# Both directions' chunk inverses merged in common groups, a longer patience for tiled groups, and the last two gMLP value blocks ahead of their input blocks

## The chip, the cores and the metric

The kernel runs on one core of one Trainium2 chip. The metric is device microseconds from start to end of the program; the time before is the median of three runs. The engines are named as the profile names them: PE is the matrix engine (PEld its weight loads), DVE the vector engine, ACT the scalar engine, POOL the general engine, SP the one that issues most DMAs.

## The reference, cut to what matters

One layer of a hybrid model runs over 640 tokens (512 of a grid and 128 of a context). One input product feeds two kinds of mixers: a bidirectional recurrence with 16 heads (RWKV-7) and a gated MLP over chunks of 128 tokens (gMLP) with 8 groups.

```python
h = _rmsnorm(x, lp['norm1_g']) * (1.0 + sc1) + sh1
p = h @ lp['w_in']
o_a, s_fin = _rwkv7_bidir(shift_fn(p[..., :C_SHIFT], lp['mu_shift']), s0, lp)
o_b = _chunk_gmlp(jax.nn.gelu(p[..., C_SHIFT:]), lp)
x = x + g1 * (jnp.concatenate([o_a, o_b], axis=-1) @ lp['w_out'])
h = _rmsnorm(x, lp['norm2_g']) * (1.0 + sc2) + sh2
ff = (jax.nn.silu(h @ lp['w_ffn_gate']) * (h @ lp['w_ffn_up'])) @ lp['w_ffn_down']
...
# _rwkv7_bidir, for each of the two directions
sa = jnp.einsum('bhvk,bhk->bhv', S, a_t)
S = S * w_t[:, :, None, :] + sa[..., None] * b_t[:, :, None, :] + v_t[..., None] * k_t[:, :, None, :]
...
# _chunk_gmlp
u, v = jnp.split(p, 2, axis=-1)
vc = v - mean
v = vc * lax.rsqrt(jnp.mean(vc * vc, axis=-1, keepdims=True) + LN_EPS) * lp['gmlp_ln_g'] + lp['gmlp_ln_b']
s = jnp.einsum('gij,bnjgd->bnigd', lp['w_spatial'], v) + lp['b_spatial'].T[:, :, None]
return (u * s.reshape(B, T, D_B)).astype(dtype)
```

## The kernel before

The program has stages. The first makes the modulation vectors for the first norm and the normalized tokens `h_hi`, `h_lo`. The second computes the input product block by block (a block is 128 columns of `w_in`) and, beside it, everything that the recurrence needs ahead of its scan, and the gMLP. The third runs the recurrence over chunks of 64 tokens with half of the output product, the later ones the rest of the output product and the feed-forward network.

In the second stage a block is 96 wide products of 128 x 128 by 320 columns on PE (`big`): 32 triples of high by high, high by low and low by high parts. 40 blocks, 1280 triples, go through the planner below. `fetch` loads a quarter of a block (`raw`), `parted` splits it (`hi`, `lo`), `take` copies the finished block out of PSUM into `praw` and appends the block's own task to a queue.

For each of eight pairs of heads p the blocks are r (`take_r`), v (`take_v`: its transposes `pvt<-ident,zv` go through the buffer `vt` to DRAM) and k (`take_k`, which makes `R` and `X` for each direction d). `tail` makes the Gram products `pG`, `solve` inverts the 16 x 16 diagonal blocks on DVE, and `merge` puts them together to inverses of 64 x 64: per direction five steps of small products on PE in 32 x 32 tiles (`pblk<-TB,A__`, `pblk<-M,TB`, `pblk<-TB,M`, `pM<-TB,GB`, `pT<-TF,M`), each followed by copies or adds out of PSUM, and at the end a store of `TF`. The blocks of gMLP group g are its value block (`take_gv`: a GELU on `praw`, transposes `pvt<-ident,praw`, a layer norm on `vt`, the weight `wspT` from `pw`) and its input block (`take_gu`: a GELU, the products `psp<-wspT,vt`, the sum `sp`, the gate, and a store to `d_o`). `mod_all` makes four more modulation vectors: 64 loads `wt` of 1 MB, each followed by one product group `pm` of four in 128 x 32 tiles; after every 16 the bias rows are loaded to `ms`, added, and transposed (`ptm`). `wt` and `ms` share one buffer.

The order of every engine is written out at build time by `Lister`, a planner with estimated costs. Each queue is a task whose instructions come in sequence (`qA`, `qR`, `qT`, `qM` for the merges, `qB` for the gMLP, and so on), and the wide products are a task that fills PE. A group of another tiling interrupts the wide products only when two such groups are ready, or one has been ready for `PATIENCE`. Once the wide products are written out, what is left is placed by the general scheduler together with the beginning of the third stage. Four accumulators in PSUM (`slots`) serve all groups but the wide ones and `pm`. Every instruction of the second stage is recorded at the line of one helper (L106 before, L109 after), so it is told apart by its tiles.

Of the kernel before, what the change touches and what calls it, by code (L numbers as in the profile page):

```python
# [10 lines left out]
F32 = mybir.dt.float32  # L11
# [8 lines left out]
P = 128  # L20
# [3 lines left out]
NT = T // P  # L24
HALF = T // 2
CH = 64
NCH = T // CH
# [21 lines left out]
SUBST = 4.6  # L49
MODR = 19.0  # L50
TOGETHER = 2
PATIENCE = 2.0
SLACK = 1.0
NREC = 8
CHK = (3, 3, 4, 4, 4, 4)
POOLK = (3,)
# [155 lines left out]


class Task:
    def __init__(self, gen, prio):
        self.gen, self.prio, self.item, self.over = gen, prio, None, False
        self.step()

    def step(self):
# [11 lines left out]
class Lister:  # L231
# [7 lines left out]
        self.wide = Task(wide, 0)  # L239
        self.tasks.append(self.wide)  # L240

    def add(self, gen, prio):
        self.tasks.append(Task(gen, prio))

    def ready(self, ops):
        e, r = ops[0].eng, 0.0
# [36 lines left out]
    def pick(self, eng, tasks):  # L283
        now = self.clock[eng]
        c = [(self.ready(t.item), t.rank(), i, t) for i, t in enumerate(tasks)]
        if eng == "PE":
            small = [x for x in c if x[3] is not self.wide and x[0] + SLACK * (x[3].item[0].tiling != self.tiling or self.tiling == (P, P)) <= now]
            wide = [x for x in c if x[3] is self.wide and x[0] <= now]
            full = [x for x in small if x[3].item[0].tiling == (P, P)]
            if full and self.tiling == (P, P):  # L290
                return now, min(full, key=lambda x: x[1])[3]
            if small and self.tiling != (P, P):
                same = [x for x in small if x[3].item[0].tiling == self.tiling]
                return now, min(same or small, key=lambda x: x[0])[3]
            if small and (not wide or len(small) >= TOGETHER or now - min(small)[0] >= PATIENCE):
                return now, min(small)[3]
            if wide:
                return now, self.wide
        start = min(max(now, x[0]) for x in c)
        return start, min((x for x in c if max(now, x[0]) <= start), key=lambda x: (x[1], x[0], x[2]))[3]  # L300
# [18 lines left out]
def flow_step(ctx: ExitStack, tc, x_prompt, x_sample, state_rwkv, c, c_ctx, w_mod, b_mod,  # L319
# [418 lines left out]
        pass  # L738

    pairs = [Pair() for _ in range(NPAIR)]  # L740

    def take_r(pr, p, read):
        o = pairs[p]
# [201 lines left out]
    vts = [None] * 8  # L945

    def take_gv(vv, g, read):
        lng, lnb, wsp = (gs.tile([P, P], F32, tag=n, name=n) for n in ("lng", "lnb", "wsp"))
        yield oQ.dma_start(lng, gmlp_ln_g[0, g].partition_broadcast(P))
        yield oQ.dma_start(lnb, gmlp_ln_b[0, g].partition_broadcast(P))  # L950
# [17 lines left out]
        va = gs.tile([P, NT], F32, name="gva")  # L968
# [61 lines left out]
    def merge(p, d2):  # L1030

        GB = pairs[p].GB
        for gq in range(8):
            b = 16 * (gq % 2)
            yield oG.dma_start(TB[16 * gq:16 * gq + 16, :, :, :, b:b + 16].rearrange("p d c w b -> p (d c w) b"),
                              d2[gq].rearrange("d c w a b -> a (d c w) b"))
        for h in range(2):
            base = 64 * (1 - h)
            for d in range(2):
                yield oS.copy(A1_[base:base + 16, d, :, 16:32], GB[d][base:base + 16, :, 16:32])  # L1040
                yield oS.copy(A1_[base + 32:base + 48, d, :, 16:32], GB[d][base + 32:base + 48, :, 48:64])
        for d in range(2):
            GBd = GB[d]
            TF = bp.tile([P, NCH, CH], F32, tag="TF", name="TF")
            for h in range(2):
                yield oG.memset(TF[hi32(h), :, 0:32], 0.0)
            Tn, TT, A1 = TB[:, d, :, 0, :], TB[:, d, :, 1, :], A1_[:, d]

            def blk(lhs, rhs, rows=range(4)):
                ps = slots.tile([P, NCH, 32], F32, "pblk")  # L1050
                four = []
                for cc in range(NCH):
                    for a_ in rows:
                        s = slice(32 * a_, 32 * a_ + 32)
                        four.append(oT.matmul(ps[s, cc, :], lhs[s, cc, :], rhs[s, cc, :], start=True, stop=True,
                                             tile_position=(32 * a_, 32 * a_)))
                return ps, four

            M1 = bp.tile([P, NCH, 32], F32, tag="M1", name="M1")
            yield slots.free  # L1060
            ps, four = blk(A1, Tn)
            yield four
            yield oS.copy(M1, ps)
            slots.done(ps)

            yield slots.free
            ps, four = blk(TT, M1, (0, 2))
            yield four
            for h in range(2):
                yield oV.tensor_add(Tn[lo32(h)], ps[lo32(h)], Tn[lo32(h)])  # L1070
            slots.done(ps)
            yield slots.free
            ps, four = blk(M1, TT)
            yield four
            for h in range(2):
                yield oV.tensor_add(TF[lo32(h), :, 0:32], ps[lo32(h)], TT[lo32(h)])
                yield oV.tensor_add(TF[hi32(h), :, 32:64], ps[hi32(h)], TT[hi32(h)])
            slots.done(ps)
            M2 = bp.tile([P, NCH, 32], F32, tag="M1", name="M2")
            yield slots.free  # L1080
            ps = slots.tile([P, NCH, 32], F32, "pM2")
            yield [oT.matmul(ps[hi32(h), cc, :], GBd[lo32(h), cc, 32:64], Tn[lo32(h), cc, :],
                            start=True, stop=True, tile_position=(64 * (1 - h), 64 * (1 - h) + 32))
                   for cc in range(NCH) for h in range(2)]
            for h in range(2):
                yield oS.copy(M2[hi32(h), :, :], ps[hi32(h), :, :])
            slots.done(ps)
            yield slots.free
            ps = slots.tile([P, NCH, 32], F32, "pT2")
            yield [oT.matmul(ps[lo32(h), cc, :], M2[hi32(h), cc, :], TF[hi32(h), cc, 32:64],  # L1090
                            start=True, stop=True, tile_position=(64 * (1 - h) + 32, 64 * (1 - h)))
                   for cc in range(NCH) for h in range(2)]
            for h in range(2):
                yield oS.copy(TF[lo32(h), :, 32:64], ps[lo32(h), :, :])
            slots.done(ps)
            yield oG.dma_start(d_S[p, :, d, :, F_T:F_T + CH], TF)
            merged.append(p)
        yield oG.memset(TB[:, :, :, 0, 0:16], 0.0)

    def mod_all():  # L1100
# [1101 lines left out]
```

## Time and profile before

| what | value |
|---|---|
| median of three runs | 3279.66 us (3274.77 to 3281.91) |
| the profiled execution | 3288.36 us, span 3286.6 us |
| mean granted clock of PE | 0.978 |
| PE busy | 3131.1 us (95%) |
| PE weight loads | 2887.5 us (88%) |
| DVE, ACT, POOL busy | 2378.6, 1441.7, 1255.7 us |
| last wide product of the second stage | issued at 1026.23 us |
| first product of the third stage | issued at 1045.21 us |

PE overlaps its matmuls, so a share of 95% does not mean that it does useful work at its peak for all of that time. A row of the order in time has its start, its duration, the engine, the line, the operation, what it writes and reads, the shape and count, and in brackets how long the engine was idle before it and what ended that. For SP and POOL queues a DMA row is the issue alone; the load lands later.

### The profile page before, as it was taken

The page shows a single profiled execution, that of the slowest core. Times are in us where ns is not written, and L with a number is a line of the kernel's source. Part 1 is how long each engine was busy: PE and PEld are TensorE (multiplying, and loading weights), DVE is VectorE, ACT ScalarE, POOL GpSimd, SP SyncE. Part 2 cuts the span into 40 slices and gives each one's busy share as a digit, 9 for nine tenths or more (in the row PEclk, how much of TensorE's full clock was granted, in tenths as well). Part 3 has the DMA queues.
Part 4 walks back from the last instruction along what each step waited for, and adds up shares of the span by engine and source line. Part 5 has one row for each costly group of instructions (what it writes and reads, how often), then busy time and mean ns, then how long its engine had stood idle before and what let it go on. Part 6 is the DMA issues. An engine that isn't in the chain of part 4 may idle for free.

```text
span 3286.6 us, 73564 instructions
## 1 busy us (share of the span) xinstructions
PE 3131.1 (95%) x28828; PEld 2887.5 (88%) x28828; DVE 2378.6 (72%) x4073; ACT 1441.7 (44%) x3161; POOL 1255.7 (38%) x1082
## 2 busy tenths in 40 slices
PE   6899999999998999899999999999999999999996
PEld 3688888889886877788899999999999999999986
DVE  4456767667665666557877888788887878877787
ACT  3244555555533333245543444444444444444365
POOL 0001222212220122310465565556655645555543
PEclk8899999999997999999999999999999999999998
DMA  8768887887895777456333333433343354554453
GB/s 316 256 181 230 218 229 206 236 217 192 236 232 171 220 231 219 124 157 181 104 115 119 120 106 120 121 116 116 110 124 120 106 175 149 157 167 128 121 167 119
DMA packets 741923, 553.01 MB, mean 168 GB/s; under 512 B 141688, under 2 KB 674184, under 8 KB 732744
## 3 DMA queue, kind: packets, MB, share of 16 engines
q1 hardware_dynamic: 729256, 534.62, 54.7%
q0 software_dynamic: 9984, 13.13, 1.7%
q8 instruction: 226, 3.70, 0.5%
q14 instruction: 121, 0.99, 0.1%
q10 hardware_dynamic: 2336, 0.57, 0.1%
HBM read 438.77 MB, written 111.69 MB: 167 GB/s over the span
## 4 chain that ended last, share of the span: by engine, by line
PE 39%; DVE 6%; issue 5%; DMA 4%; ACT 1%; POOL 1%; DVEq 0%; SPq 0%; ACTq 0%; POOLq 0%
PE P L1816 13%; PE P L1815 12%; PE P L1814 12%; DVE lo L1633 3%; DMA d_os<-act 2%; DVE act L1935 1%; DMA opd<-d_op 1%; ACT hi L1632 1%; DVE xd L1867 0%; PE big L1669 0%; PE big L1668 0%; PE big L1667 0%; DVE xo L1596 0%; PE C L1748 0%; DVE out L2170 0%
## 5 line engine op out<-in xcount | busy, mean ns | idle before, releaser
L1816 PE MATMUL P<-xo,lo 128*128 128x320 f32 x2352 | 732.8, 312 | 13.5 <-DVE lo L1633 13.4
L1814 PE MATMUL P<-xo,hi 128*128 128x320 f32 x2352 | 729.6, 310 | 6.9 <-ACT hi L1632 6.9
L1815 PE MATMUL P<-xo,hi 128*128 128x320 f32 x2352 | 728.4, 310 | 0.0
L1633 DVE TENSOR_TENSOR lo<-raw,hi 128x512 fp32r<-128x512 f32 x532 | 574.9, 1098 | 78.2 <-ACT hi L1632 73.3
L1632 ACT CAST hi<-raw 128x512 fp32r<-128x512 f32 x532 | 326.3, 621 | 414.1 <-PE P L1815 320.1
L1816 PEld LDWEIGHTS P<-xo,lo 128*128 128x128 f32 x2352 | 443.1, 188 | 22.6 <-DVE lo L1633 22.6
L1814 PEld LDWEIGHTS P<-xo,hi 128*128 128x128 f32 x2352 | 443.2, 188 | 9.4 <-ACT hi L1632 9.1
L1815 PEld LDWEIGHTS P<-xo,hi 128*128 128x128 f32 x2352 | 443.1, 188 | 0.0
L106 PE MATMUL big<-h_hi,hi 128*128 128x320 f32 x1280 | 419.3, 328 | 1.0 <-ACT praw L1209 1.0
L1727 POOL TENSOR_TENSOR raw<-raw 128x512 f32<-128x512 f32 x252 | 408.5, 1631 | 11.6 <-DVE lo L1633 1.6
L1816 PE MATMUL P<-xd,lo 128*128 128x320 f32 x1232 | 384.8, 312 | 16.3 <-DVE lo L1633 16.1
L106 PE MATMUL big<-h_lo,hi 128*128 128x320 f32 x1280 | 395.2, 309 | 0.0
L106 PE MATMUL big<-h_hi,lo 128*128 128x320 f32 x1280 | 395.1, 309 | 0.0
L1814 PE MATMUL P<-xd,hi 128*128 128x320 f32 x1232 | 382.7, 311 | 6.2 <-ACT hi L1632 4.1
L1815 PE MATMUL P<-xd,hi 128*128 128x320 f32 x1232 | 381.3, 309 | 0.0
L1632 ACT CAST hi<-rawd 128x512 fp32r<-128x512 f32 (+1 forms) x288 | 168.9, 588 | 239.3 <-PE P L1815 204.6
L1727 POOL TENSOR_TENSOR t<-raw 128x512 f32<-128x512 f32 x84 | 135.6, 1615 | 358.9 <-DMA raw<-in_w_ffn_up_dram 352.0
L106 PEld LDWEIGHTS big<-h_hi,hi 128*128 128x128 f32 x1280 | 241.8, 189 | 32.9 <-issue 26.1
L1816 PEld LDWEIGHTS P<-xd,lo 128*128 128x128 f32 x1232 | 231.9, 188 | 24.0 <-DVE lo L1633 23.5
L106 PEld LDWEIGHTS big<-h_lo,hi 128*128 128x128 f32 x1280 | 241.8, 189 | 1.3 <-issue 0.2
L106 PEld LDWEIGHTS big<-h_hi,lo 128*128 128x128 f32 x1280 | 241.1, 188 | 0.0
L1633 DVE TENSOR_TENSOR lo<-rawd,hi 128x512 fp32r<-128x512 f32 (+1 forms) x288 | 221.8, 776 | 26.1 <-ACT hi L1632 22.3
(370 smaller groups left out, 6275.9 us busy)
## 6 DMA issues: line engine op xcount, KB each, us to landing
wt<-in_w_mod_dram SPq DMA_DIRECT2D x96, 1024.0 KB
raw<-in_w_ffn_gate_dram SPq DMA_DIRECT2D x182, 256.0 KB
raw<-in_w_ffn_up_dram SPq DMA_DIRECT2D x182, 256.0 KB
rec<-d_S SPq DMA_DIRECT2D x80, 576.0 KB
raw<-in_w_in_dram SPq DMA_DIRECT2D x172, 256.0 KB
rawd<-in_w_ffn_down_dram SPq DMA_DIRECT2D x128, 256.0 KB
raw<-in_w_out_dram SPq DMA_DIRECT2D x96, 256.0 KB
xd<-d_os SPq DMA_DIRECT2D x66, 320.0 KB
```

Of the source, the lines that this page charges most:

```text
L106: self.eng, self.run = eng, lambda: fn(*args, **kw)
L1632: S.copy(hi[:, 0:nk], raw[:, 0:nk])
L1633: V.tensor_sub(lo[:, 0:nk], raw[:, 0:nk], hi[:, 0:nk].bitcast(F32))
L1727: G.tensor_tensor(out=o[:, 0:nk], in0=p[:, 0:nk], in1=q[:, 0:nk], op=ALU.subtract)
L1814: TE.matmul(ps, hi[:, k, :], xk[:, 0, :], start=f, stop=False)
L1815: TE.matmul(ps, hi[:, k, :], xk[:, 1, :], start=False, stop=False)
L1816: TE.matmul(ps, lo[:, k, :], xk[:, 0, :], start=False, stop=l)
L1935: V.tensor_sub(lo, src, hi.bitcast(F32))
```

## The change

Merging runs once per pair. Each of the five steps of `merge` issues the products of both directions as one group, into two accumulators taken together, and the copies and adds of both follow; the two `TF` buffers are `TF` and `vt`, which the value transposes of `take_v` use too, so a list `held` lets only one of the two users in at a time. `PATIENCE` goes from 2 to 3 for all tasks (it becomes a property of a task, with the same value for all). In `take_gv` the offset `lnb` is loaded later, into the buffer of `wsp`, and group 7 gets buffers of its own for `wspT` and `vt`, the latter once all pairs have passed. The blocks of groups 6 and 7 come in the order value 6, value 7, input 6, input 7.

```diff
-PATIENCE = 2.0
+PATIENCE = 3.0
+PACE = 3.0
+PATM = 3.0
+PATT = 3.0
...
-            if small and (not wide or len(small) >= TOGETHER or now - min(small)[0] >= PATIENCE):
+            if small and (not wide or len(small) >= TOGETHER or any(now - x[0] >= x[3].patience for x in small)):
...
+        yield lambda: not held
+        held.append(p)
         vt = bp.tile([P, NT, P], F32, tag="vt", name="vt", bufs=1)
         yield from turned(o.zv, vt, "pvt")
         yield oQ.dma_start(d_vt[p, 0].rearrange("(q t) v -> t q v", t=P), vt)
+        held.pop()
...
-        wspT = gs.tile([P, P], F32, name="wspT")
+        wspT = (bk if g == 7 else gs).tile([P, P], F32, tag="wlr" if g == 7 else "wspT", name="wspT", bufs=1)
         yield oS.copy(wspT, pw[:, 0, :])
         slots.done(pw)
-        vt = bp.tile([P, NT, P], F32, tag="vt2", name="vt2", bufs=1)
+        lnb = gs.tile([P, P], F32, tag="wsp", name="lnb")
+        yield oQ.dma_start(lnb, gmlp_ln_b[0, g].partition_broadcast(P))
+        if g == 7:
+            yield lambda: done["zv"] == NPAIR
+        vt = bp.tile([P, NT, P], F32, tag="t2" if g == 7 else "vt2", name="vt2", bufs=1)
...
-        for d in range(2):
-            GBd = GB[d]
-            TF = bp.tile([P, NCH, CH], F32, tag="TF", name="TF")
...
+        two = lambda: [slots.tile([P, NCH, 32], F32, "pblk") for d in range(2)]
+
+        def blk(ps, lhs, rhs, rows=range(4)):
+            return [oT.matmul(ps[d][s, cc, :], lhs[d][s, cc, :], rhs[d][s, cc, :], start=True, stop=True,
+                             tile_position=(s.start, s.start))
+                    for d in range(2) for cc in range(NCH) for s in (slice(32 * a_, 32 * a_ + 32) for a_ in rows)]
+
+        yield slots.pair
+        ps = two()
+        yield blk(ps, [A1_[:, d] for d in range(2)], Tn)
...
+        yield lambda: not held
+        held.append(p)
+        TF = [bp.tile([P, NCH, CH], F32, tag=n, name="TF", bufs=1) for n in ("TF", "vt")]
...
+        held.pop()
...
         while g < GORD[p]:
-            block(CSH + DA + P * g, take_gv, g, qB)
-            block(CSH + P * g, take_gu, g, qB)
-            g += 1
+            both = (g, g + 1) if g == 6 else (g,)
+            for u in both:
+                block(CSH + DA + P * u, take_gv, u, qB)
+            for u in both:
+                block(CSH + P * u, take_gu, u, qB)
+            g += len(both)
...
-        plan.add(queue(qT), 2)
+        plan.add(queue(qT), 2, PATT)
...
-        plan.add(queue(qM), 3)
+        plan.add(queue(qM), 3, PATM)
...
-        plan.add(mod_all(), 5)
+        plan.add(mod_all(), 5, PACE)
```

How the order moves is seen at three places. The first is PE in the middle of the second stage, at the fourth step of the first pair's merge. `pR` and `pXT` are transposes of other tasks, and a number at the end of a name is the buffer's. Before:

```order
L106 MATMUL pR<-ident,rb 128x128 x4
L106 MATMUL big<-h_hi,hi 128x320
L106 MATMUL big<-h_lo,hi 128x320
L106 MATMUL big<-h_hi,lo 128x320
L106 MATMUL pM_3923<-TB,GB 32x32 x20
L106 MATMUL pXT<-ident,X 128x128 x4
```

The same step of the changed kernel, on PE:

```order
L109 MATMUL big<-h_hi,lo 128x320
L109 MATMUL pm_3612<-wt,cT 2x512 x4
L109 MATMUL pblk<-TB,GB 32x32 x40
L109 MATMUL pXT<-ident,X 128x128 x4
L109 MATMUL big<-h_hi,hi 128x320
```

One direction's 20 products stood alone between full products; now 40 of both directions follow a modulation group, which has a tiling of its own too.

The second place is PE at the end of the second stage, from the last wide products on. Before:

```order
L106 MATMUL pT_13681<-TF,M_13649 32x32 x20
L106 MATMUL big<-h_hi,hi 128x320
L106 MATMUL big<-h_lo,hi 128x320
L106 MATMUL big<-h_hi,lo 128x320
L106 MATMUL pw<-ident,wsp 128x128
L106 MATMUL pvt_13759<-ident,praw 128x128 x4
L106 MATMUL pvt_13765<-ident,praw 128x128
L106 MATMUL psp<-wspT,vt_13758 128x128 x5
```

The same place of the changed kernel, where `vt_13357` is group 6's and `vt_13697` group 7's:

```order
L109 MATMUL big<-h_hi,lo 128x320
L109 MATMUL pblk<-TB,GB 32x32 x40
L109 MATMUL pblk<-TF,M_13577 32x32 x40
L109 MATMUL pm_10641<-wt,cT 2x512 x4
L109 MATMUL pw<-ident,wsp 128x128
L109 MATMUL pvt_13698<-ident,praw 128x128 x4
L109 MATMUL pvt_13704<-ident,praw 128x128
L109 MATMUL psp<-wspT,vt_13357 128x128 x5
L109 MATMUL pm_10641<-wt,cT 2x512 x4
L109 MATMUL psp<-wspT,vt_13697 128x128 x4
L109 MATMUL ptm<-ident,ms_13718 128x128 x4
L109 MATMUL psp<-wspT,vt_13697 128x128
```

Before, group 7's transposes and its product were all that stood behind the last wide product; now the merge's last two steps, two modulation groups with their transposes and group 6's product stand there too.

The third place is DVE at the same end. `L1315` (L1331 after) and the `ST` copy are the third stage's. Before, from the last step of group 7's norm on:

```order
L106 TENSOR_TENSOR vt_13758<-vt_13758,lnb 128x640
L106 TENSOR_TENSOR gq<-gq,praw 128x640
L1315 TENSOR_TENSOR gq<-gr,gq 32x640
L106 SCALAR_TENSOR_TENSOR praw<-gq,praw 128x640
L106 TENSOR_TENSOR sp<-psp,bsp 128x512
L106 TENSOR_TENSOR sp<-psp,bsp 128x128
L106 SCALAR_TENSOR_TENSOR praw<-praw,sp 128x640
L1353 COPY ST<-swap 128x128
```

The changed kernel, from just behind the same step:

```order
L109 SCALAR_TENSOR_TENSOR praw<-gq,praw 128x640
L1331 TENSOR_TENSOR gq<-gr,gq 32x640
L109 TENSOR_TENSOR ms_13718<-pm_10641,ms_13718 2x512 x4
L109 TENSOR_TENSOR sp<-psp,bsp 128x512
L109 TENSOR_TENSOR sp<-psp,bsp 128x128
L109 SCALAR_TENSOR_TENSOR praw<-praw,sp 128x640
L109 COPY modc_86<-ptm 128x16 x2
L109 TENSOR_SCALAR gq<-gq 128x640
L109 TENSOR_TENSOR gq<-gq,praw 128x640
L109 SCALAR_TENSOR_TENSOR praw<-gq,praw 128x640
L109 TENSOR_TENSOR sp<-psp,bsp 128x512
L109 TENSOR_TENSOR sp<-psp,bsp 128x128
```

Before, one GELU's end and one `sp` followed the norm; now the four `ms` adds, group 6's `sp`, and group 7's whole GELU stand ahead of the last `sp`.

More of the change, by code (lines that the diff above doesn't have):

```diff
@@ L214, with __init__ @@
 class Task:
-    def __init__(self, gen, prio):
-        self.gen, self.prio, self.item, self.over = gen, prio, None, False
+    def __init__(self, gen, prio, patience=0.0):
+        self.gen, self.prio, self.patience, self.item, self.over = gen, prio, patience, None, False
         self.step()
@@ L240, in __init__, with add @@
         self.tasks.append(self.wide)
-    def add(self, gen, prio):
-        self.tasks.append(Task(gen, prio))
+    def add(self, gen, prio, patience=PATIENCE):
+        self.tasks.append(Task(gen, prio, patience))
     def ready(self, ops):
@@ L740, in flow_step @@
     pairs = [Pair() for _ in range(NPAIR)]
+    held = []
     def take_r(pr, p, read):
@@ L947, in take_gv @@
     def take_gv(vv, g, read):
-        lng, lnb, wsp = (gs.tile([P, P], F32, tag=n, name=n) for n in ("lng", "lnb", "wsp"))
+        lng, wsp = (gs.tile([P, P], F32, tag=n, name=n) for n in ("lng", "wsp"))
         yield oQ.dma_start(lng, gmlp_ln_g[0, g].partition_broadcast(P))
-        yield oQ.dma_start(lnb, gmlp_ln_b[0, g].partition_broadcast(P))
         yield oQ.dma_start(wsp, w_spatial[0, g])
@@ L967, in take_gv @@
         yield oS.activation(sq, vt, AF.Square)
-        va = gs.tile([P, NT], F32, name="gva")
+        va = gs.tile([P, NT], F32, tag="gmn", name="gva")
         yield oV.tensor_reduce(out=va, in_=sq, axis=AX.X, op=ALU.add)
@@ L1041, in merge @@
                 yield oS.copy(A1_[base + 32:base + 48, d, :, 16:32], GB[d][base + 32:base + 48, :, 48:64])
-        for d in range(2):
-            GBd = GB[d]
-            TF = bp.tile([P, NCH, CH], F32, tag="TF", name="TF")
-            for h in range(2):
[L1046 to L1068, printed above, removed]
-            for h in range(2):
[L1070 to L1074, printed above, removed]
-            for h in range(2):
[L1076 to L1084, printed above, removed]
-            for h in range(2):
[L1086 to L1092, printed above, removed]
@@ new lines, in merge @@
+        Tn, TT = ([TB[:, d, :, w, :] for d in range(2)] for w in range(2))
+        M1 = bp.tile([P, 2, NCH, 32], F32, tag="M1", name="M1")
+        TF = [None] * 2
+        two = lambda: [slots.tile([P, NCH, 32], F32, "pblk") for d in range(2)]
[3 more added lines that the diff above has]
+                    for d in range(2) for cc in range(NCH) for s in (slice(32 * a_, 32 * a_ + 32) for a_ in rows)]
@@ new lines, in merge @@
+        yield slots.pair
+        ps = two()
+        yield blk(ps, [A1_[:, d] for d in range(2)], Tn)
+        for d in range(2):
+            yield oS.copy(M1[:, d], ps[d])
+            slots.done(ps[d])
+        yield slots.pair
+        ps = two()
+        yield blk(ps, TT, [M1[:, d] for d in range(2)], (0, 2))
+        for d in range(2):
+            for h in range(2):
+                yield oV.tensor_add(Tn[d][lo32(h)], ps[d][lo32(h)], Tn[d][lo32(h)])
+            slots.done(ps[d])
+        yield lambda: not held
@@ new lines, in merge @@
+        held.append(p)
+        TF = [bp.tile([P, NCH, CH], F32, tag=n, name="TF", bufs=1) for n in ("TF", "vt")]
+        for d in range(2):
+            for h in range(2):
+                yield oG.memset(TF[d][hi32(h), :, 0:32], 0.0)
+        yield slots.pair
+        ps = two()
+        yield blk(ps, [M1[:, d] for d in range(2)], TT)
+        for d in range(2):
+            for h in range(2):
+                yield oV.tensor_add(TF[d][lo32(h), :, 0:32], ps[d][lo32(h)], TT[d][lo32(h)])
+                yield oV.tensor_add(TF[d][hi32(h), :, 32:64], ps[d][hi32(h)], TT[d][hi32(h)])
+            slots.done(ps[d])
@@ new lines, in merge @@
+        M2 = bp.tile([P, 2, NCH, 32], F32, tag="M1", name="M2")
+        yield slots.pair
+        ps = two()
+        yield [oT.matmul(ps[d][hi32(h), cc, :], GB[d][lo32(h), cc, 32:64], Tn[d][lo32(h), cc, :],
+                        start=True, stop=True, tile_position=(64 * (1 - h), 64 * (1 - h) + 32))
+               for d in range(2) for cc in range(NCH) for h in range(2)]
+        for d in range(2):
+            for h in range(2):
+                yield oS.copy(M2[hi32(h), d], ps[d][hi32(h), :, :])
+            slots.done(ps[d])
@@ L1093, in merge @@
+        yield slots.pair
+        ps = two()
+        yield [oT.matmul(ps[d][lo32(h), cc, :], M2[hi32(h), d, cc, :], TF[d][hi32(h), cc, 32:64],
+                        start=True, stop=True, tile_position=(64 * (1 - h) + 32, 64 * (1 - h)))
+               for d in range(2) for cc in range(NCH) for h in range(2)]
+        for d in range(2):
             for h in range(2):
-                yield oS.copy(TF[lo32(h), :, 32:64], ps[lo32(h), :, :])
-            slots.done(ps)
-            yield oG.dma_start(d_S[p, :, d, :, F_T:F_T + CH], TF)
+                yield oS.copy(TF[d][lo32(h), :, 32:64], ps[d][lo32(h), :, :])
+            slots.done(ps[d])
+            yield oG.dma_start(d_S[p, :, d, :, F_T:F_T + CH], TF[d])
```

## The prediction

> **What bounds the kernel now.** I read the page first (busy shares, slices, granted clock), then busy time by stretches of the second stage, then the instructions in order of time at one tiled group and at the end of the stage, then the waits on the tiles that the change touches.
>
> ```profile
> PE 3131.1 (95%) x28828; PEld 2887.5 (88%) x28828; DVE 2378.6 (72%) x4073; ACT 1441.7 (44%) x3161; POOL 1255.7 (38%) x1082
> ...
> PE   6899999999998999899999999999999999999996
> ...
> PEclk8899999999997999999999999999999999999998
> ```
>
> TensorE (PE) is busy nearly everywhere; slice 13 (986 to 1068 us), with a clock of 7 tenths, holds the end of the second stage, the only stage that the change rewrites. Its stretches:
>
> ```profile
> 450.00:550.00 100.00, 97.61 (x1438) 84.62 (x1437) 70.89 (x152) 50.93 (x112) 23.38 (x37) 0.98 0.83 225
> 650.00:750.00 100.00, 96.80 (x1243) 84.88 (x1241) 65.50 (x140) 48.34 (x106) 23.06 (x37) 0.97 0.79 213
> 850.00:950.00 100.00, 98.09 (x1540) 84.61 (x1542) 67.35 (x155) 46.89 (x104) 24.88 (x40) 1.00 0.85 228
> 950.00:1026.00 76.00, 73.57 (x1138) 65.78 (x1133) 46.70 (x84) 28.92 (x60) 14.10 (x21) 0.98 0.71 184
> 1026.00:1046.00 20.00, 4.84 (x23) 3.87 (x23) 14.88 (x23) 7.78 (x15) 2.19 (x2) 0.63 0.77 254
> ```
>
> The columns are window, length, busy PE, weight loads, DVE, ACT, POOL, clock, DMA share, GB/s. Up to 1026 us the stage is PE's own issue time: the first four windows leave it idle for only 2.39 + 3.20 + 1.91 + 2.43 = 9.9 us. The last 20 us are a tail in which PE works 4.84 us. So the change can pay in two ways: less PE issue time in the body, or a shorter tail.
>
> The tail, in order of time:
>
> ```profile
> 1025.56 0.74 ACT L106 ACTIVATE gq<-praw 128x640 f32<-128x640 f32 x1 [1.93 <-DVE praw L106]
> 1026.23 0.31 PE L106 MATMUL big<-h_hi,lo 128*128 128x320 f32 x1
> ...
> 1028.67 0.82 DVE L106 SCALAR_TENSOR_TENSOR praw<-gq,praw 128x640 f32<-128x640 f32 x1
> ...
> 1029.65 0.74 PE L106 MATMUL pvt<-ident,praw 128*128 128x128 f32 x5 [2.76 <-DVE praw L106]
> ...
> 1040.91 0.82 DVE L106 TENSOR_TENSOR vt<-vt,lnb 128x640 f32<-128x640 f32 x1
> ...
> 1041.88 2.48 PE L106 MATMUL psp<-wspT,vt 128*128 128x128 f32 x10 [11.50 <-DVE vt L106]
> ...
> 1044.27 0.89 DVE L106 TENSOR_TENSOR sp<-psp,bsp 128x512 f32<-128x512 f32 x2
> ...
> 1045.21 1.11 PE L1537 MATMUL pxT<-ident,x1T 128*128 128x128 f32 x4 [0.85 <-DVE sp L106]
> ```
>
> The last wide product issues at 1026.23. The value block of group 7 is then activated (1025.56 to 1029.49: 3.9 us for a GELU), transposed, normalized (1029.65 to 1041.73: 12.1 us) and multiplied; the third stage begins when the sum `sp` is done at 1045.16, which is 18.8 us after the wide products (1026.38).
>
> **Merges in common groups, and longer patience.** No instruction is added or taken away; both edits regroup. A tiled group among wide products costs this:
>
> ```profile
> 377.31 0.30 PE L106 MATMUL big<-h_lo,hi 128*128 128x320 f32 x1
> ...
> 377.45 0.31 PE L106 MATMUL big<-h_hi,lo 128*128 128x320 f32 x1
> 377.69 0.71 PEld L106 LDWEIGHTS pM<-TB,GB 32*32 32x32 f32 x40 [0.19 <-issue]
> 377.69 0.82 PE L106 MATMUL pM<-TB,GB 32*32 32x32 f32 x40
> 378.44 0.42 PEld L106 LDWEIGHTS pXT<-ident,X 128*128 128x128 f32 x4
> ```
>
> Wide products start 0.145 us apart, the tiled group 0.24 after one: 0.09 to enter. Its 40 loads began within 0.60 us, the next full load 0.15 after the last: 0.13 to leave. I take 0.2 for going out and back, since part of the exit is the group's own streaming, and 0.1 from one tiling to another. Counted in the order of instructions, 152 excursions become 126, and 70 changes between tilings become 55: 26 x 0.2 + 15 x 0.1 = 6.7 us less PE time. Ends: entry alone, 26 x 0.09 = 2.3; both sides in full, 26 x 0.22 + 15 x 0.13 = 7.7.
>
> Patience delays each tiled step by up to 1 us, and a merge now needs two free accumulators per step. What is queued behind is that direction's own chain, while wide products fill PE; this is free as long as wide products last. Its price is lateness: in the order, the last Gram group stands 47 wide triples (of 1280) later than before, and what is late then falls into the tail. The mutual exclusion `held` makes pair p's value transposes wait for a merge's last buffer; on PE they move by up to 60 triples, also under wide products: nothing there. `lnb` is now loaded after the transposed weight has left `wsp`, and `bsp`, in the same buffer, after `lnb`'s last reader: two small loads per group that SP issues later, with the weight loads behind them in its queue. Wide products run from loads up to three pieces ahead, so I cost them at nothing in the body; without that lead each would cost at most the wait that it makes on SP. Group 7's own buffers (`wlr`, `t2`) only free it from group 6's readers. The wait for `done["zv"]` holds only queue B, whose remainder is the tail.
>
> **The tail after the change.** In the order, after the last wide product, there now stand both merges' last two steps, two modulation products with their loads one after the other in one buffer, group 7's value block as before, and in addition group 6's product. Nothing of the value block moved ahead of the end. The first place to cost is the modulation.
>
> ```profile
> 961.97 0.39 SPq L106 DMA_DIRECT2D wt<-in_w_mod_dram  x1
> ...
> 972.55 1.04 PE L106 MATMUL pm<-wt,cT 128*2 128x512 f32 x8 [0.50 <-DMA wt<-in_w_mod_dram]
> ...
> 979.33 0.38 SPq L106 DMA_DIRECT2D wt<-in_w_mod_dram  x1
> ...
> 985.59 1.04 PE L106 MATMUL pm<-wt,cT 128*2 128x512 f32 x8 [1.42 <-DMA wt<-in_w_mod_dram]
> ...
> 1009.59 0.53 POOL L106 MEMSET ms<- 128x512 f32 x1 [1.37 <-PE pm L106]
> ...
> 1012.25 2.08 SPq L106 DMA_DIRECT2D ms<-in_b_mod_dram  x6
> ...
> 1016.96 0.67 DVE L106 TENSOR_TENSOR ms<-pm,ms 2x512 f32<-2x512 f32 x1
> ...
> 1019.56 2.12 DVE L106 TENSOR_TENSOR ms<-pm,ms 2x512 f32<-2x512 f32 x3
> ```
>
> Both products waited for their load, so a load takes 10.6 or 6.3 us from issue; I take 8.5, between two equally near rows. From the memset's end (1010.12) to the first add are 6.8 us, the four adds take 2.8.
>
> ```profile
> L106 DVE TENSOR_TENSOR TF<-pblk,TB x64: 478/484/499, 373.2 to 1019.1; 32x320 f32<-32x320 f32 x64
> ...
> who waited for it (us, times):
> ...
>   PEld pG L106: 0.9, 1
>   PEld pM L106: 0.2, 1
> ```
>
> With 0 at the end of the last wide product: product 62 ends at -2.6 (behind it one merge group of some 1.6 us, an estimate from the 0.75 above, and six wide products of 0.145). Load 63 is there at +6.1. PE reaches product 63 only after the last merge step, which needs all eight `TF` adds: on DVE these stand behind four `TB` adds and group 6's normalization (from about -6.5: 1.9 for the adds, six operations of 0.83, 1.7 for POOL's power and small ones), so they run from +2.1 to +6.0. The step takes 1.5, product 63 ends at about +9.2. Load 64 lands at +17.9, its product ends at +19.4, and with 0.5 + 6.8 + 2.8 the adds end at +29.5. DVE's order puts them ahead of group 6's `sp` (0.89) and gate (0.83); then come group 7's GELU (3.9) and `sp` (0.89): +36.0. The value chain alone is looser: transposes at +9.5, 12.1 to the last `lnb`, 2.5 for three more operations, +24.1, while the first `ms` add can start at +26.7; `bsp`'s load, which may go at +21.6, has seven microseconds before its reader. So the tail grows from 18.8 to 36.0, by 17.2.
>
> What moved there leaves the body: four merge steps of 0.75, two products of 1.04, ten `psp` at half of 2.48: 6.3. **Sum:** 17.2 - 6.3 - 6.7 = +4.2 us. Against the profiled execution (3288.36, span 3286.6) that is 3292.6; it stands 8.7 above the median of the runs, 3279.66, to which I carry the difference: 3284. Ends from load times alone: with 6.3 the adds come 2.2 earlier, +2.0; with 10.6 for both, 2.8 later, +7.0. With the switch ends +3.2 to +8.6.
>
> [...]
>
> **Rivals.** A, faster: the extra microsecond of patience lets operands arrive, and PE's waits in the body go. For it: waits of 0.50 and 1.42 for loads above, 9.9 us idle in all. Against it: the order spaces the products no wider. Half of the 9.9, and a tail without the wait for the adds (29, from product 63 at +5 and load 6.3), give 4.2 - 5 - 7 = -8: 3272. It decides from 10.8 us below my sum: with the last `sp` at +25, or with some of it there and some in the body.
>
> B, slower: the two late loads share the queue and the DMA engines with the third stage's records (share 0.77 in the tail, above), and the eight bias rows wait behind records on SP. Both loads at 10.6 and 3 us more for the rows: +10, 3290. It decides from 2.4 us more than my sum.
>
> C, slower: both directions' results are now taken out of PSUM in one go, and each of the eight merges makes PE wait for its eight adds (3.9 us, of which I let other work fill two): 15 us more, 3299. Against it stand the 1.1 us of such waits above, with the adds four at a time.
>
> D: the switches cost nothing that the grouping saves, or waits like the next one eat it: +4.2 + 6.7, 3291.
>
> ```profile
> 731.53 1.22 PE L106 MATMUL pG<-R,X 64*64 64x128 f32 x17 [2.74 <-issue]
> ...
> 728.00:732.00 4.00, 1.26 (x46) 0.98 (x36) 0.00 (x0) 0.43 (x1) 0.00 (x0) 0.84 0.91 227
> 732.00:738.00 6.00, 6.00 (x69) 4.95 (x62) 3.75 (x7) 3.01 (x6) 0.00 (x0) 0.54 0.36 110
> ```
>
> One such wait costs its 2.74 us and then half of the 6 us at clock 0.54, some 5.7 in all. [...]
>
> **Chances.** Forecast (3284, own range 3275 to 3286) 0.42; A 0.25; B 0.23; C 0.05; D 0.05. About 0.2%, 6.6 us, is what a measurement of this kernel can tell from no change. So faster 0.25, same 0.42, slower 0.33. The range reaches down past A and up past D: 3270 to 3293.
>
> **What would show it.** Right: in the changed profile the last wide product issues some 13 us earlier, about 1013; after it two modulation products 9 to 11 us apart; eight `TF` adds just before the last merge step; the third stage's first product at about 1049. Wrong: the first transposes of group 7 start within 5 us of the last wide product, `ms` adds never wait, or idle PE time before the last wide product falls below 3 us or exceeds 20. What would break the sum is body waits that the order cannot show.

## The result and the profile after

| | before | after |
|---|---|---|
| median | 3277.94 us (3274.77 to 3281.91, 4 runs) | 3314.23 us (3309.42 to 3317.19, 4 runs) |
| profiled execution, span | 3288.36, 3286.6 us | 3313.0, 3311.1 us |
| last wide product | 1026.23 us | 1037.21 us |
| first product of the third stage | 1045.21 us | 1068.99 us |

The ratio is 1.0113 (95% interval 1.0094 to 1.0131): 36 us slower, where +4 was forecast and 3293 was the upper end. The profiled pair is only 24.5 us apart, since the profiled execution of the kernel before was some 10 us longer than the median of its runs. Of these 24.5 us 23.8 lie in the second stage (1068.99 - 1045.21); what follows took 2241.4 and 2242.1 us there. Over the ten profiled kernels of the experiments that remainder, which none of them changes, lay between 2226.9 and 2237.5. So I compare the end of the second stage first, and times only beside it. One profile does not give the stage's loss to better than some 8 us: e8 below, the changed kernel moved by one whole block of instructions, takes the same time, and in its profile the stage ends at 1076.84, 31.6 us after the kernel before.

The page of the changed kernel:

```profile
PE 3134.2 (95%) x28828; PEld 2895.7 (87%) x28828; DVE 2382.8 (72%) x4073; ACT 1443.4 (44%) x3161; POOL 1253.8 (38%) x1082
...
PE   6899999999997999999999999999999999999996
...
PEclk8999999999997999999999999999999999999998
```

It hardly differs from the page before: the same work at the same rates. The stage cut into stretches says more (window, length, busy PE, weight loads, DVE, ACT, POOL, clock, DMA share, GB/s):

```profile
650.00:750.00 100.00, 100.00 (x1404) 87.80 (x1403) 68.94 (x146) 51.87 (x114) 23.38 (x37) 1.00 0.82 221
850.00:950.00 100.00, 93.88 (x1545) 82.55 (x1546) 67.50 (x144) 47.77 (x105) 26.84 (x42) 0.98 0.81 201
950.00:1037.00 87.00, 79.92 (x1102) 70.27 (x1101) 47.99 (x102) 33.88 (x71) 18.73 (x29) 0.94 0.79 200
1037.00:1069.00 32.00, 14.86 (x219) 10.65 (x217) 23.73 (x42) 10.59 (x21) 4.00 (x5) 0.65 0.70 217
```

PE is full from 650 to 750 us and idle for 6.1 of 100 us from 850, where it was idle for 1.9 before; the clock falls to 0.94 in the last stretch of the body (the part of the stage up to the last wide product). One place in the order of time:

```profile
927.11 0.38 PE L109 MATMUL pXT<-ident,X 128*128 128x128 f32 x2
927.42 1.58 PE L109 MATMUL pblk<-TB,A__1111 32*32 32x32 f32 x160
928.93 0.79 PE L109 MATMUL pW<-Z,GA 64*64 64x64 f32 x19
933.89 0.26 PE L109 MATMUL pW<-Z,GA 64*64 64x64 f32 x1 [4.18 <-issue]
```

PE stops inside a group. The trace counts these small fp32 products as two records each, so the 80 products of a common merge step stand as x160 and the ten `pW` products as twenty. Of these twenty records, which read the same two buffers and fill one accumulator, nineteen run and the last waits 4.18 us for "issue", that is for nothing that the profile can name. The stretches of this wait, and the DMA queues in two pieces of it, 929.7 to 931.4 first and then 931.4 to 932.6 us (queue, kind: packets, MB, share):

```profile
926.00:929.70 3.70, 3.70 (x190) 3.37 (x189) 2.18 (x3) 1.22 (x3) 0.00 (x0) 1.00 0.73 192
929.70:933.90 4.20, 0.02 (x2) 0.00 (x0) 1.00 (x2) 0.00 (x0) 0.00 (x0) 0.98 1.04 302
933.90:940.00 6.10, 6.10 (x90) 5.48 (x91) 3.08 (x6) 2.36 (x5) 0.00 (x0) 0.73 0.66 204
```

```profile
q1 hardware_dynamic: 848, 0.40, 85.2%
q14 instruction: 1, 0.01, 1.1%
...
q1 hardware_dynamic: 975, 0.34, 118.9%
q8 instruction: 1, 0.02, 5.5%
```

The first piece has no packet of the instruction queue q8, the second has one: it begins at 931.48 us, 1.8 us after PE has run dry, and PE goes on 2.41 us later. Over the whole program the page counts the same queue:

```profile
q8 instruction: 226, 3.70, 0.5%
```

PE executes 28828 products and as many weight loads. 57656 instructions in 226 packets are 255 for each, so one packet brings about 128 records with their loads. No view names the engine that q8 serves; this count, and the packets with which the waits below end, tie it to PE. PE went through the 128 records ahead of this wait in 1.9 us (927.86 to 929.72), where 128 wide products at 0.145 us last 18.6.

In all, the second stage after the change has eleven such waits above 0.6 us, 23.6 us together (20.4 of them ahead of the last wide product); before there were two, 4.0 us. Each of the eleven ended 2.2 to 2.7 us after a q8 packet began, and 3.3 to 7.4 us after PE had passed the record 128 places earlier. The trace also has periods in which the granted clock is one half, of 3.4 to 10.2 us each. In the body they rose from three (6.8 us lost) to six (17.1 us lost). Not all of them stand at a wait for the fetch: two of the three before (3.4 us lost) and the longest of the six after (5.1 us lost) began during or right behind a wait for a load `wt` (2.30 and 1.42 us before, 4.85 us after).

### The profile page after: what moved, and what is told of

Read it like the earlier page. It is cut to its first block, busy times and chain, and to the rows that moved or that the text cites. A ratio compares the mean times of both kernels' runs of the same rounds, so it can differ in the third digit from the quotient of the medians.

```text
span 3311.1 us, 73591 instructions
## 1 busy us (share of the span) xinstructions
PE 3134.2 (95%) x28828; PEld 2895.7 (87%) x28828; DVE 2382.8 (72%) x4073; ACT 1443.4 (44%) x3161; POOL 1253.8 (38%) x1082
## 4 chain that ended last, share of the span: by engine, by line
PE 41%; DVE 6%; DMA 4%; issue 4%; ACT 1%; POOL 0%; DVEq 0%; SPq 0%; ACTq 0%; POOLq 0%
PE P L1832 13%; PE P L1830 13%; PE P L1831 13%; DVE lo L1649 2%; DMA d_os<-act 2%; DMA opd<-d_op 1%; DVE act L1951 1%; ACT hi L1648 1%; DVE xd L1883 0%; PE big L1685 0%; PE big L1683 0%; PE big L1684 0%; PE C L1764 0%; PE C L1762 0%; PE C L1763 0%
```

## The experiments

The theory: **a common merge step issues 160 records back to back. With what the planner chains to it (8 to 40 records of `pG`, `pW` or `pm`) a run reaches 200 records, more than one fetch block, and lasts some 1.6 to 3.6 us, which is mostly less than the 3.3 to 7.4 us after which PE went on above. Wide products between short groups (128 last 18.6 us) hide the same fetch.** The rivals: the waits belong to those groups themselves (two accumulators at once, operands, DMA neighbours), or the loss is the late tail that longer patience and the new gMLP order bring.

### The same program, moved against the fetch blocks

Three kernels are the changed kernel with extra products on unused cells of `pc`, in the first 12 us, where PE waits for DVE. There are 54 in e1, 18 in e2 and 64 in e8, and they move everything behind them by 108, 36 and 128 records.

```diff
         TE.transpose(pc[:, 0, 0:32], crow, ident[0:32, 0:32])
+        for _ in range(18):
+            TE.matmul(pc[0:32, 1, 0:32], ident[0:32, 0:32], ident[0:32, 0:32], start=True, stop=True)
```

> The changed kernel with 54 extra 32x32 products in PE's idle time near 9 us; everything else as it is. They move PE's instruction stream by 108 records against the blocks in which it is fetched. Theory (PE runs through a common group of 160 records faster than the next 128-record block of instructions arrives): the waits without a releaser in the second stage depend on where the block limits fall. With 4.5 us from the limit before to the next block being there, worked out on the changed kernel's own trace, 5 stalls of 10 us together are left of 11 with 23.6 us, at the groups near 362, 383, 544, 566 and 1036 us; the ones near 785, 841, 875 and 934 us go. Time 13 + 6 x 1.5 us (half clock after each stall) less: about 3292. Rival (the waits belong to those groups: their PSUM, their operands, their DMA neighbours): the same eleven groups wait, 23 us, and the time stays at 3314.

> The same with 18 extra products (36 records), by the theory a bad place for the block limits: 12 stalls, 31 us, among them groups that did not wait before (near 472, 661, 679 and 758 us) and none near 362 and 566 us; time 8 us more than the changed kernel, about 3322. Rival (the waits belong to the groups): no change, 3314, the same eleven groups.

> The changed kernel with 64 extra 32x32 products in PE's early idle time: 128 records, one whole fetch block. Theory: the limits fall in the same places of the program as in the changed kernel, so the same groups wait (362, 551, 566, 841, 934, 1042 us and so on), 20 to 27 us, and the stage ends at 1069; against 54 and 18 extra products this tells the products' own cost from that of the place. Rival (any extra product at the start loosens the program): stalls and stage end differ from the changed kernel as much as with 54 or 18.

| extra records | time | ratio | waits | end of stage 2 |
|---|---|---|---|---|
| 0 (the change) | 3314.23 | 1.0113 [1.0094, 1.0131] | 11, 23.6 us | 1068.99 |
| 108 (e1) | 3303.11 | 1.0067 [1.0041, 1.0092] | 9, 19.1 us | 1061.86 |
| 36 (e2) | 3306.38 | 1.0086 [1.0062, 1.0109] | 11, 28.5 us | 1076.11 |
| 128 (e8) | 3313.86 | 1.0105 [1.0085, 1.0124] | 11, 29.4 us | 1076.84 |

The place that was shown above, in e2, then in e1, then in e8, in the order of time:

```profile
935.69 1.56 PE L109 MATMUL pblk<-TB,A__1129 32*32 32x32 f32 x143
940.97 0.44 PE L109 MATMUL pblk<-TB,A__1129 32*32 32x32 f32 x17 [3.72 <-issue]
```

```profile
924.93 1.58 PE L109 MATMUL pblk<-TB,A__1165 32*32 32x32 f32 x160
926.44 0.80 PE L109 MATMUL pW<-Z,GA 64*64 64x64 f32 x20
927.17 0.33 PE L109 MATMUL pvt<-ident,praw 128*128 128x128 f32 x1
...
931.68 0.81 PE L109 MATMUL pmm<-fs,bones 128*128 128x320 f32 x2 [1.54 <-issue]
```

```profile
936.46 1.58 PE L109 MATMUL pblk<-TB,A__1175 32*32 32x32 f32 x160
937.97 0.79 PE L109 MATMUL pW<-Z,GA 64*64 64x64 f32 x19
943.13 0.26 PE L109 MATMUL pW<-Z,GA 64*64 64x64 f32 x1 [4.37 <-issue]
```

In the changed kernel the wait came after 160 + 19 = 179 records of this run. With 36 records ahead of it, it comes after 143 = 179 - 36, in the middle of the merge step. With 108 it comes 20 records later (128 - 108), past the tiled run, and has shrunk to 1.54 us. With 128 it stands at the same product again. Counted from the program's start it is the same place each time: in the changed kernel PE goes on at records 5172, 8344, 9102, 10372 and 11898 among others, and in e2 at these same five numbers, although other products stand there. In e8 all eleven waits of the changed kernel are there again, each at the same product, which now stands 128 records later. So the waits belong to the block limits and not to a group, which rules out the rival of operands, accumulators or neighbours.

Not all of the forecasts held. The groups that e1 was to lose at 785 and 875 us did lose their waits, and those kept at 362, 566 and 1036 did wait. Those at 383 and 544 did not; those at 841 and 934 kept a wait right behind the run (1.99 and 1.54 us); and the sum is 19.1 us and not 10. A likely reason is that the delay of a block was taken as 4.5 us throughout, where the trace has 3.3 to 7.4. The time fell by 11 and not by 22. In e2 the groups near 472, 661, 679 and 758 us waited, or the products right behind them, which had not, and those at 362 and 566 no longer, as said. Its stage ends 7 us later, but the median is 3306 and not 3322; the profiled execution is the slowest of its four (3313.71), and the sum of waits in the others is not known. In e8 the sum is 29.4 us, above the 20 to 27 that were forecast, and the stage ends at 1076.84 and not at 1069: the places are the same, but the waits there differ (4.46 us where the changed kernel had 1.13, for one). The positions carry the verdict here, not these times.

### Runs shorter than a block

```diff
-        yield blk(ps, [A1_[:, d] for d in range(2)], Tn)
+        one = blk(ps, [A1_[:, d] for d in range(2)], Tn)
         for d in range(2):
+            yield one[40 * d:40 * d + 40]
             yield oS.copy(M1[:, d], ps[d])
...
-        yield blk(ps, [M1[:, d] for d in range(2)], TT)
+        one = blk(ps, [M1[:, d] for d in range(2)], TT)
         for d in range(2):
+            yield one[40 * d:40 * d + 40]
             for h in range(2):
```

> The changed kernel with the two merge steps of 160 records (first and third) yielded per direction again, 80 and 80, with the planner free to put wide products between; the shorter three steps stay common. Theory: the longest tiled run falls from 200 to 120 records, less than one block of 128; the block model gives 13 us of stalls as a mean over all places of the limits, against 25 for the changed kernel, so 5 to 16 us. Four modulation products stand behind the last wide product (changed kernel: two), so the tail grows by some 14 us and eats what the body gains: last wide product near 1025, time 3305 to 3315. Rival (the waits come with common groups as such, their two accumulators or their operands): 11 stalls with 20 us or more.

3287.38 us, ratio 1.0031 [1.0017, 1.0045]: of the 36 us that the change costs, 27 are gone, with everything else of the change in place. Not all 27 are the fetch's: the waits for `wt` in the body (5.5 us in the changed kernel) are gone too. Three waits with 4.3 us are left. The body from 150 us to the last wide product, in the changed kernel and then in this one:

```profile
150.00:1037.30 887.30, 860.32 (x11169) 762.35 (x11167) 577.30 (x1204) 424.36 (x916) 186.27 (x295) 0.98 0.79 207
```

```profile
150.00:1003.50 853.50, 846.30 (x11154) 753.23 (x11154) 580.99 (x1211) 425.92 (x918) 185.83 (x295) 1.00 0.80 213
```

Idle PE time falls from 27.0 to 7.2 us, the clock rises from 0.98 to 1.00, and the last wide product comes 33.7 us earlier. The tail grew to 44.1 us (expected: about 46), so the stage ends at 1047.58. The time forecast of 3305 to 3315 was too high: the last wide product was expected near 1025, and the waits fell to 4.3 us, not to the mean of 13 over all places of the limits (4.3 lies just below the 5 to 16 that were forecast). Whether the limits fell well or the model asks for too much was not tried.

### The parts of the change alone

Common merges alone (the three new patience values and the gMLP order set back):

> Common merge groups alone: patience back at 2.0 everywhere, the gMLP blocks in the old order. Theory: the runs of 160 to 200 tiled records are all there, so about 11 stalls with 20 to 27 us and the half clock after them; less 5 us for switches: +26 against the kernel before, about 3304. Rival (what costs is the late tail, from patience and the order of the gMLP blocks): few stalls and at most 3284.

3298.46 us, 1.0056 [1.0034, 1.0079], +19.3 against 3279.14 on the same chip, where +26 was forecast: ten waits for the fetch, 22.4 us, all in the body, and 13.7 us lost to the half clock. An eleventh wait marked "issue" (2.91 us, in the tail) ends when the `ms` adds do, 31 us after the last q8 packet, and is none for the fetch. The last wide product is issued at 1035.60. It needs neither the patience nor the new order to go wrong.

Patience alone (`PATIENCE = 3.0` in the kernel before):

> The kernel before with PATIENCE 3.0 alone, merges per direction. Theory: the longest tiled run stays at 122 records, so at most 3 stalls with under 6 us; what it costs is its tail, where six modulation products now stand behind the last wide product, each with its own load (6 to 10 us) in one buffer: up to +25, about 3300, all of it after the last wide product and none before it. Rival (longer patience itself chains groups until PE outruns its fetch): 6 stalls or more in the body.

3280.66 us, 1.0007 [0.9995, 1.002]: no difference. There is no wait for the fetch in the body, the clock never falls there, and the last wide product is issued at 998.90 us, 27 us earlier than before. The tail takes it back; the stage ends at 1051.75:

```profile
998.90 0.30 PE L106 MATMUL big<-h_hi,lo 128*128 128x320 f32 x1
...
1009.40 1.89 PE L106 MATMUL pm<-wt,cT 128*2 128x512 f32 x8 [4.95 <-DMA wt<-in_w_mod_dram]
...
1018.28 1.89 PE L106 MATMUL pm<-wt,cT 128*2 128x512 f32 x8 [2.90 <-DMA wt<-in_w_mod_dram]
1027.26 1.89 PE L106 MATMUL pm<-wt,cT 128*2 128x512 f32 x8 [7.09 <-DMA wt<-in_w_mod_dram]
...
1043.03 1.89 PE L106 MATMUL pm<-wt,cT 128*2 128x512 f32 x8 [7.04 <-DMA wt<-in_w_mod_dram]
...
1051.75 0.66 PE L1537 MATMUL pxT<-ident,x1T 128*128 128x128 f32 x2 [0.44 <-DVE modc L106]
```

Modulation products wait for their loads one after the other and start 7 to 9 us apart. The expected 3300 missed the gain in the body, the expected tail of loads came.

The gMLP order alone (with its buffers and locks; merges per direction, patience 2.0):

> The new order of the gMLP blocks with its buffers and locks, but merges per direction as before and patience 2.0. Theory: no run of tiled records above 124, so at most 3 stalls and under 6 us of them in the body; the last wide product near 1022 us. Behind it five modulation products stand in the order, each with its own load, where the kernel before has none: a tail near 45 us, so about +20, 3298. Rival (the common merges are the whole loss): 3279, the tail stays near 19.

3285.79 us, 1.0023 [1.0013, 1.0034], +7.6. Two waits for the fetch (2.5 us), last wide product at 1018.10, tail 39.1 us. It costs something, by the tail (expected near 45), but less than the forecast 20. The three parts alone add up to 19.3 + 1.5 + 7.6 = 28 of the 36 us.

### What patience buys without the loads in the tail

The kernel before, with patience per task as in the change, 3.0 for all but the modulation:

```diff
-PATIENCE = 2.0
+PATIENCE = 3.0
+PACE = 0.0
...
-        plan.add(mod_all(), 5)
+        plan.add(mod_all(), 5, PACE)
```

> The kernel before with patience 3.0 for all tiled steps but the modulation products, which get 0 and so aren't kept back. Theory: as with patience alone no stalls in the body (longest run 122 records, block model 1.3 us) and the last wide product near 1003 us, 4 us later than there for 18 more switches; but no modulation product stands behind it, so the tail is no chain of loads: the last merge steps and group 7's value block, 19 to 24 us as in the kernel before. The stage ends near 1025, 20 us before: about 3259. Rival (the tail of patience alone is merge and gMLP work, its loads only fill it): tail 45 us or more, 3280.

3263.99 us, ratio 0.9964 [0.9952, 0.9977]: faster than both kernels. The body, and the tail in the order of time:

```profile
150.00:1007.90 857.90, 856.03 (x11157) 754.12 (x11155) 585.66 (x1221) 429.10 (x924) 188.26 (x297) 1.00 0.80 218
```

```profile
1007.82 0.31 PE L109 MATMUL big<-h_hi,lo 128*128 128x320 f32 x1
...
1025.50 2.47 PE L109 MATMUL psp<-wspT,vt 128*128 128x128 f32 x10 [8.94 <-DVE vt L109]
...
1028.62 0.66 PE L1540 MATMUL pxT<-ident,x1T 128*128 128x128 f32 x2
```

PE is idle for 1.9 of 857.9 us, with no wait for the fetch and the full clock, and the tail is 20.8 us, the value block of group 7 as in the kernel before. The forecast was 3259, 5 us too low, and near the lowest of its runs (3258.51 to 3275.92).

Two versions put the new gMLP order on top of it (merges still per direction), to shorten that last tail:

> Merges per direction, patience 3.0, modulation products never kept back, and the new order of the gMLP blocks: all of the change but the common groups, with the loads taken out of the tail. Theory: no tiled run above 116 records, so no stalls worth 3 us; behind the last wide product stand only one 40-record merge step and the two spatial products, no load and no value block, so the tail falls from 21 (modulation first, old gMLP order) to about 10 us, and the last wide product stands near 1011: the stage ends at 1021, time 3257. Rival (the new gMLP order costs by itself, as it did alone with +7.6): 3272, with waits in the body or a tail above 25.

> The same with patience 3.5 and the merges at 2.0: all merge steps stand ahead of the last wide product, only the two spatial products (20 records) behind it. Longest run 122, 17 runs above 100 records, block model 2.0 us. Theory: last wide product near 1015, tail 8: 3260, within 5 us of the version with 3.0. Rival (more runs just under a block's length already cost): 4 stalls or more, 3270.

3278.72 us (1.0006 [0.9996, 1.0016]) and 3280.84 us (1.0011 [0.9997, 1.0025]): 3257 and 3260 were forecast. The gain of e7 is gone, as the rival of e9 had it, which gave 3272. The last wide products are issued at 1023.67 and 1024.19, the tails are 18.7 and 17.2 us. Only 1.6 and 1.2 us in the two bodies are waits for the fetch; waits for the load `wt` are 9.6 and 6.9 us, where e7 had 0.6. In e9 these 9.0 us more, the 1.6 and 3.4 us lost to the half clock make 14.0 of the 15.9 us by which its last wide product comes after e7's. In the changed kernel, e1, e2, e5 and e8, which share the new order, waits on loads above 0.6 us in the body come to 5.5 to 10.7 us, in the kernels with the old order to at most 3.7; e6 is the exception (new order, 1.3). That the order makes these loads late is likely by this, and why was not tried. The tail that was to fall to 10 us did not. The trace of e9 shows what filled it: group 7's norm runs in it up to 1030.71; only then can `bsp`, which now follows `lnb` in one buffer, be loaded (issued at 1030.74); group 6's `sp` waits 2.69 us for it, and group 7's GELU stands between it and the last `sp` at 1041.42.

## Why the prediction was wrong

By its own steps, for the end of the second stage: forecast +4.2 us, measured +23.8.

- **The step that failed: "No instruction is added or taken away; both edits regroup", with the body's waits taken over unchanged.** The order showed x80 groups where there were x40, and the prediction priced only the entries and exits that this saves. What it left out is how long PE can issue at 9 ns a record (160 in 1.51 us at 927.42) before its instructions run out. The waits for the fetch in the body rose by 16.5 us (from 4.0 to 20.4), half-clock periods took 10.2 us more (from 6.8 to 17.1), and waits for `wt` 1.8 more. Together 28.5 us. By the wait at which each period began, 8.5 of the 10.2 us belong to the fetch and 1.7 to `wt`, so about 25 us are the fetch's. The moved kernels show that the block limits place the fetch's waits, the split one that most of them need the long runs.
- The trace of before had the sign of it: the wait of 2.74 us at 731.53 was quoted, in a run of `pblk` x80 and `pG` x32. Rival D named "waits like the next one" but priced no more than the lost switches (6.7 us, about one such wait), with a chance of 0.05. Asking what that "issue" wait stood behind, a tiled run of nearly a fetch block, would have given the warning: sixteen runs of 128 records and more between wide products in the new order, none in the old.
- **Switches and moved work:** forecast -13.0 us in the body. What is left of the measured +11.0 without the 28.5 is -17.5. If nothing else is in that remainder, this step was right in sign and 4.5 us too small.
- **The tail:** forecast from 18.8 to 36.0 us after the end of the last wide product, measured 31.6. Its rows:

```profile
1037.21 0.31 PE L109 MATMUL big<-h_hi,lo 128*128 128x320 f32 x1
...
1041.88 0.34 PE L109 MATMUL pblk<-TB,GB 32*32 32x32 f32 x10 [3.17 <-issue]
...
1044.42 1.89 PE L109 MATMUL pm<-wt,cT 128*2 128x512 f32 x8
...
1046.37 0.36 SPq L109 DMA_DIRECT2D wt<-in_w_mod_dram  x1
...
1052.05 1.04 PE L109 MATMUL pm<-wt,cT 128*2 128x512 f32 x8 [2.14 <-DMA wt<-in_w_mod_dram]
...
1059.55 2.84 DVE L109 TENSOR_TENSOR ms<-pm,ms 2x512 f32<-2x512 f32 x4
...
1068.05 0.89 DVE L109 TENSOR_TENSOR sp<-psp,bsp 128x512 f32<-128x512 f32 x2
...
1068.99 1.12 PE L1553 MATMUL pxT<-ident,x1T 128*128 128x128 f32 x4 [0.91 <-DVE sp L109]
```

  Product 63 ends 9.0 us after the last wide product's end (forecast 9.2), though part of that is a wait for the fetch; the next load takes 5.7 us where 8.5 was taken; the four adds end at +25.0 (29.5), and GELU and `sp` follow. The chain is the one that was described, and the largest term that was off is the load time, too long by 2.8 us.
- **Of the rivals**, A (the body's waits go) is what patience does alone, in e4 and e7, though the waits that go there are mostly the fetch's (4.0 to 0 us in e4) and less those for operands (3.7 to 2.3). B was wrong in its place: late loads cost 1.8 us of waits more in the body, and in the tail the load took 5.7 us, less than the 8.5 that were taken. C, the copies out of PSUM as the bound, is not seen: the waits move with the block limits and mostly go when the runs are split, while both accumulators are still taken together.
- Of the signs for the forecast, the last wide product near 1013 and the third stage's first product near 1049 did not come (1037.21 and 1068.99). Of the signs against it, idle PE time above 20 us before the last wide product came true (27.0), and so did the last sentence, on body waits that the order cannot show.

## What to carry to other kernels

Beside what a group of small products saves in switches, count its instructions. Here a packet of the fetch brought about 128 records; about half of the 16 runs of 160 to 200 records without long products between had a wait for it in them or right behind, and at all six waits for it of 2.0 us and more, or within 2 us behind them, the granted clock went to one half. Such waits were marked "issue" in the middle of a group, came at the same instruction count whatever stood there, and fell from eleven (23.6 us) to three (4.3 us) when the longest runs were halved and long products could go between. And a change that makes the body faster must be judged with its tail: the 27 us that patience won in the body were lost to loads that had slipped behind the last wide product, and keeping those loads early turned no gain into 14 us.

## What the hardware showed that was not expected

- At its eleven waits the changed kernel's PE went on 3.3 to 7.4 us after it had passed the record 128 places earlier, and 2.2 to 2.7 us after a packet of about 255 instructions began. Runs of 90 to 122 records between wide products nearly always hid this (16 of them in the body of the kernel before, two waits); of the 16 runs of 160 to 200 records in the body after the change about half had a wait in them or right behind.
- Waits of 2 to 5 us were mostly enough for a half-clock period. In the changed kernel's stage all six waits for the fetch of 2.0 us and more have one, at their end or within 2 us of it, and the four of 0.97 to 1.27 us that stand outside of such a period have none; the wait of 4.85 us for `wt` has one too. It is no sharp limit: a wait of 2.32 us for `wt` in e4 has none, one of 1.42 us in the kernel before has one. The 6.1 us after the wait of 4.18 us ran at a mean clock of 0.73.
